# Roots of the down stage's first half taken ahead of its stores and of the next loads on GpSimd's queue

## The chip, the cores and the metric

The kernel runs on one core of one Trainium2 chip. The metric is the time of one execution on the device in microseconds (us), from the first instruction to the last; runs are compared by their median. The profile shows one further execution, taken instruction by instruction.

A core has five engines, each of which works through its own list of instructions in order: PE (TensorE, matrix products into the PSUM banks), DVE (VectorE), ACT (ScalarE), POOL (GpSimd) and SP (SyncE, which here only issues transfers). They wait for one another through semaphores. A DMA that an engine issues is carried out by the 16 DMA engines. SP's transfers stand in the profile as queue q1, POOL's as queue q0.

## The reference

A block of a language model in float32: 1024 rows of width 1024, a mixer of two branches, a feed-forward part with a short convolution, and a last normalisation. What matters here is its end:

```python
def rms_norm(x, g):
    xf = x.astype(jnp.float32)
    y = xf * lax.rsqrt(jnp.mean(xf * xf, axis=-1, keepdims=True) + EPS)
    return (y * g.astype(jnp.float32)).astype(x.dtype)

def conv_ffn(h, w_up, conv_w, conv_b, w_down):
    u = causal_dwconv(h @ w_up, conv_w, conv_b)
    gate, up = jnp.split(u, [D_FF], axis=-1)
    return (jax.nn.silu(gate) * up) @ w_down
...
    h = h + conv_ffn(rms_norm(h, norm_ffn[l]), ffn_w_up[l], ...)
    h = rms_norm(h, norm_final)
    return h[:, N_META:, :]
```

The last three lines are what the stage in question computes: the product with `w_down`, the sum with `h`, and the normalisation of each row.

## The kernel before

The kernel goes through its stages once: normalisation and projections, the heads of the two branches, their merge and the output product, the up product, and the down product with the final normalisation. Only the last one, the down stage, is touched.

**The down stage.** It multiplies the activations (1024 x 2816) by `w_down` (2816 x 1024) in a two-by-two block scheme with seven block products in place of eight. The rows of the output are made in two halves, r = 0 and r = 1. Each half has two phases, and each phase runs over 11 steps m; so there are 44 steps in the list `seq`, numbered 0 to 43. Step 22 is the first of the second half. In the first phase a step is 24 products of 128x128 by 128x512, eight groups of three, into the banks V, X, Y and Z for the row blocks j = 0 and j = 1. Steps 22 and 23 and steps 31 and 32 are run in pairs: j = 0 of both, and then j = 1 of both.

**Operands.** Each step has three operands: raw weights (`rd`), made weights (`tdn`) and activations (`adr`), in the first phase 512 KB each. `fill` (line 1732) fetches them with SP and splits each for the matrix unit into a rounded part (ACT, line 1752, `ACTIVATE`) and a rest (DVE, line 1753, `TENSOR_TENSOR`). The tile of a step is named by its home in memory, `db`, `do` or `dw`, and by the step's number: step 27 is `dw`, step 28 `db`, steps 29, 30 and 31 `do` with `dy` for the activations, step 32 `db` again. Eight homes are used in turn, so operands are fetched some steps ahead; a fetch waits until PE is through with the step whose home it takes.

**Rows.** The output rows of a half stand in four tiles `accs` of 128x1024. They come in from `hsc` (the values h), take up the banks' sums, and are normalised: `finish` (line 1849) adds the sums, squares (ACT, line 1858), makes the mean (DVE, `fv`, lines 1862 and 1864), the root (POOL, `fr`, line 1866, a power of -0.5), multiplies by the weights `gfin` (DVE, line 1871), scales by the root (ACT, line 1872) and stores the row block to `out` (line 1874). In the first half, roots, scaling and stores are put off: `later` keeps them until step 24, two steps into the second half, and the stores go out on POOL. The four loads of the next rows (`load_acc`, line 1838, POOL too) take the same four tiles, so each must wait until the store from its tile has landed.

**What sets the order.** The order on every engine is fixed when the program is built: instructions are taken by priority (`hp(n)` raises it) as their inputs are expected to be ready, so what is written in one loop is interleaved with the splitting of operands on ACT and DVE. `tc.issue_after(ins)` keeps what is issued inside it on `ins`'s engine behind `ins`.

Of the kernel before, what the change touches and what calls it, by code (L numbers as in the profile page):

```python
# [9 lines left out]
F32 = mybir.dt.float32  # L10
# [3 lines left out]
OP = mybir.AluOpType  # L14
# [3 lines left out]
P = 128  # L18
# [27 lines left out]
def hybrid_kernel(ctx, tc, x, meta, norm_mix, w_in, b_in, gla_w_gate, gla_b_gate, gla_norm,  # L46
                  ml_conv_w, ml_conv_b, ml_norm, w_branch_gla, w_branch_ml, w_out, norm_ffn,
                  ffn_w_up, ffn_conv_w, ffn_conv_b, ffn_w_down, norm_final, out):
    nc = tc.nc
    x, out = x[0], out[0]  # L50
# [8 lines left out]
    def hp(n):  # L59

        return tc.high_priority(offset=max(1, min(n, tc.cur_priority - floor[0])))

    const = ctx.enter_context(tc.tile_pool(name="const", bufs=1))
# [18 lines left out]
    mhalf = const.tile([P, 1], F32, name="mhalf")  # L82
# [5 lines left out]
    rooted, flipped = [], {}  # L88
# [79 lines left out]
    class Units:  # L168
# [3 lines left out]
        def add(self, *spec):  # L172
            self.specs.append(spec)
            return len(self.specs) - 1
# [166 lines left out]
    def norm_x(i):  # L341
        n = NM if i == 0 else P
        c0 = 0 if i == 0 else NM + P * (i - 1)
        xt = xts[i]
        ss = hd.tile([P, 1], F32, name=f"xss{i}", tag="ss1", bufs=3)
        junk = hd.tile([P, T], F32, name=f"xj{i}", tag="of", bufs=2)
        nc.scalar.activation(junk[:n, :D], xt[:n, :D], AF.Square, accum_out=ss[:n])
        with hp(40):
            v = hd.tile([P, 1], F32, name=f"xv{i}", tag="xv", bufs=3)
            nc.vector.tensor_scalar(v[:n], ss[:n], 1.0 / D, EPS, OP.mult, OP.add)  # L350
            rs = hd.tile([P, 1], F32, name=f"xr{i}", tag="xr", bufs=3)
            last = nc.gpsimd.tensor_tensor(rs[:n], v[:n], mhalf[:n], OP.pow)
        nc.vector.scalar_tensor_tensor(xt[:n, :D], xt[:n, :D], rs[:n], gmix[:n], OP.mult, OP.mult)
        for g in range(2):
            tp = ps.tile([P, 4, P], F32, name=f"xtp{i}_{g}", tag="pj" if i == 1 else "s", bufs=3)
            for j in range(4):
                k = 4 * g + j
                nc.tensor.transpose(tp[:, j, :n], xt[:n, k * P:(k + 1) * P], ident[:n, :n])
            with hp(40):
                h4 = xH[:, 4 * g:4 * g + 4, c0:c0 + n]  # L360
                rounded = nc.scalar.activation(h4, tp[:, :, :n], AF.Copy)
                l4 = xL[:, 4 * g:4 * g + 4, c0:c0 + n]
                nc.vector.tensor_tensor(l4, tp[:, :, :n], h4.bitcast(F32), OP.subtract)
        return last, rounded
# [38 lines left out]
    for i in range(5, NC + 1):  # L403
        last, _ = norm_x(i)
# [890 lines left out]
    def load_o(g, pool, tags, queue):  # L1295

        t = {}
        for p in "HL":
            for i in range(2):
                tag, shape = f"{tags}{p}{i}", [P, 4, NP]  # L1300
                t[p, i] = pool.tile(shape, F32R, name=f"o{g}{p}{i}", tag=tag)
        for k in range(NK):
            h, l = (t[p, k // 4][:, k % 4, :NP] for p in "HL")
            last = queue.dma_start(l.bitcast(F32), otd[g][k])
            split = nc.scalar.activation(h, l.bitcast(F32), AF.Copy)
            nc.vector.tensor_tensor(l, l.bitcast(F32), h.bitcast(F32), OP.subtract)
        return tuple([t[p, k // 4][:, k % 4, :] for k in range(NK)] for p in "HL"), last, split
# [43 lines left out]
    for j in range(NK):  # L1351
# [7 lines left out]
        if j == 1:  # L1359
            with tc.issue_after(opened.ins), tc.issue_after(loaded.ins):  # L1360
                om_, loaded, _ = load_o("m", r1b, "R", nc.gpsimd)
# [61 lines left out]
    for p in "HL":  # L1423
        t = rb.tile([P, 28, W0], F32R, name=f"B{p}0", tag=f"B{p}0")
# [403 lines left out]
    t = r2.tile([P, 4, D], F32, name="accs", tag="OL1")  # L1828
# [4 lines left out]
    def acc_of(r, j):  # L1833
        return accs[j], accs[2 + j]

    def load_acc(r, load, n):
        j, i = divmod(n, 2)
        return lambda: load(acc_of(r, j)[i], hsc[4 * i + 2 * r + j])
# [4 lines left out]
    def middle(r, j):  # L1843

        a, b = acc_of(r, j)
        with hp(400 if j == 0 else 200):
            for acc, h, x in ((a, lo, "X"), (b, hi, "Y"), (b, hi, "Z"), (a, lo, "V")):
                add(acc, h, banks[r, j, x])

    def finish(r, j):  # L1850
        acc = acc_of(r, j)
        end = (r, j) == (1, 1)
        if end:
            f0 = rb.tile([P, T], F32, name="f0", tag="T12")[:, :D]
        ss = [const.tile([P, 3], F32, name=f"fss{r}{j}{i}", tag=f"fs{i}", bufs=2) for i in range(2)]

        def square(i, n):
            return nc.scalar.activation(junk, acc[i][:, (lo, hi)[n]], AF.Square, accum_out=ss[i][:, n:n + 1])

        def root(i, cols=None):  # L1860
            v = const.tile([P, 1], F32, name=f"fv{r}{j}{i}", tag="hv", bufs=2)
            nc.vector.tensor_scalar(v, ss[i][:, i:i + 1], 1.0 / D, EPS, OP.mult, OP.add)
            for c in cols or [1 - i]:
                mean = nc.vector.scalar_tensor_tensor(v, ss[i][:, c:c + 1], 1.0 / D, v, OP.mult, OP.add)
            rs = const.tile([P, 1], F32, name=f"fr{r}{j}{i}", tag="hr", bufs=2)
            nc.gpsimd.tensor_tensor(rs, v, mhalf, OP.pow)
            return rs, mean

        def scaled(i):
            rs, _ = root(i)  # L1870
            nc.vector.tensor_tensor(acc[i], acc[i], gfin, OP.mult)
            nc.scalar.activation(acc[i], acc[i], AF.Copy, scale=rs)
            t = 4 * i + 2 * r + j
            (nc.sync if r else nc.gpsimd).dma_start(out[P * t:P * (t + 1), :], acc[i])

        with hp(400 if j == 0 else 200):
            for i, h in ((1, hi), (0, hi), (1, lo)):
                add(acc[i], h, banks[r, j, "X"])
            square(1, 1)
            square(0, 0)  # L1880
            if end:
                nc.vector.tensor_tensor(fo[:, hi], acc[1][:, hi], gfin[:, hi], OP.mult)
                nc.vector.tensor_tensor(f0[:, lo], acc[0][:, lo], gfin[:, lo], OP.mult)
            add(acc[0], hi, banks[r, j, "Y"])
            square(0, 1)
            if end:
                rs0, _ = root(0)
                nc.vector.tensor_tensor(f0[:, hi], acc[0][:, hi], gfin[:, hi], OP.mult)
            elif r:
                scaled(0)  # L1890
            if end:
                for c, q in zip((0, 2), QUARTERS):
                    nc.vector.tensor_tensor(acc[1][:, q], banks[r, j, "Z"][:, q], acc[1][:, q], OP.add)
                    squared = nc.scalar.activation(junk[:, q], acc[1][:, q], AF.Square, accum_out=ss[1][:, c:c + 1])
            else:
                add(acc[1], lo, banks[r, j, "Z"])
                square(1, 0)
                if r:
                    scaled(1)
                else:  # L1900
                    later.append(scaled)
                return
        with tc.issue_after(squared.ins):
            nc.scalar.activation(f0, f0, AF.Copy, scale=rs0)
        t = 2 * r + j
        nc.sync.dma_start(out[P * t:P * (t + 1), :], f0)
        rs, mean = root(1, (0, 2))
        with tc.issue_after(mean.ins):
            nc.vector.tensor_tensor(fo[:, lo], acc[1][:, lo], gfin[:, lo], OP.mult)
        t = NC - 1  # L1910
        nc.scalar.activation(fo[:, lo], fo[:, lo], AF.Copy, scale=rs)
        nc.scalar.dma_start(out[P * t:P * (t + 1), lo], fo[:, lo])
        nc.vector.tensor_scalar(fo[:, hi], fo[:, hi], rs, None, OP.mult)
        nc.sync.dma_start(out[P * t:P * (t + 1), hi], fo[:, hi])

    AHEAD, PRI_F, ACC_AT = 4, 100, 7
# [26 lines left out]
    back, later = [], []  # L1943
    i = FIRST
    while i < len(seq):
        r, ph, m = seq[i]
        k = i % NP2
        if k == 0 and ph == 0:
            open_round(r)

        n = 4 if (r, ph, k) == (1, 1, NP2 - 4) else 2 if k in (0, NP2 - 2) else 1
        ahead(i + n - 1)
        if later and k == 2:
            for whole in later:
                for x in range(2):
                    whole(x)
            later.clear()
        if (r, ph, k) == (1, 0, 5):
            with hp(PRI_F):
                for n4 in range(4):  # L1960
                    load_acc(r, nc.gpsimd.dma_start, n4)()
        end = i + n == len(seq)
        for j in range(2):
            if end and j:
                for b, c in (("X", lo), ("Y", lo), ("Z", QUARTERS[0]), ("Z", QUARTERS[1])):
                    for x in range(n):
                        down(i + x, j, b, c)
            else:
                for x in range(n):
                    down(i + x, j)  # L1970
            if k + n == NP2:
                (finish if ph else middle)(r, j)
        i += n
# [29 lines left out]
```

## Time and profile before

| | us |
|---|---|
| three runs | 1873.92, 1877.96, 1879.45 |
| median | 1877.96 |
| the profiled execution | 1881.06 |
| its span, first to last instruction | 1879.3 |
| PE busy in the span | 1848.5 (98%) |
| DVE busy | 1222.6 (65%) |
| ACT busy | 869.6 (46%) |
| POOL busy | 424.4 (23%) |

All times inside the profile count from the start of the span. The down stage's second half begins near 1755. A row of a timeline gives start, duration, engine, line, operation, result and sources, and in brackets the idle time of the engine just before and what ended it. A row of the windows gives the busy time of the engines in a stretch, then the clock granted to PE, the share of the DMA engines and their rate. A queue's row gives packets, MB, and the share of 16 engines that the packets took.

### The profile page before, as it was taken

The numbers are of one execution on the slowest core, as the hardware profiler recorded it, in microseconds if no ns is written. First come the engines' busy times: TensorE is split into PE (matmuls) and PEld (weight loads), VectorE is DVE, ScalarE is ACT, GpSimd is POOL, SyncE is SP. The second block draws the span as 40 slices with busy tenths as digits, with TensorE's granted clock in tenths as the row PEclk, the third lists the DMA queues.
The fourth block names the chain that finished last, engine by engine and source line by source line (L and its number), as shares of the span: only waits on it lengthen the run. The fifth ranks groups of instructions, "written<-read, shape, count | busy, mean of one in ns | idle before, by whom it ended". The sixth has DMA issues, their size and how long they took to land.

```text
span 1879.3 us, 32613 instructions
## 1 busy us (share of the span) xinstructions
PE 1848.5 (98%) x13284; PEld 1769.7 (94%) x13284; DVE 1222.6 (65%) x1813; ACT 869.6 (46%) x1395; POOL 424.4 (23%) x476
## 2 busy tenths in 40 slices
PE   8999999999999999999999999999999999999988
PEld 7899999999999999999999999999999999977866
DVE  7766756655552566655533547788878888787776
ACT  6565555645544434332512335444434434365664
POOL 5201101205441001142381600023222222100100
PEclk8999999999999999999999999999999999999999
DMA  5111022144223655665963733333333343298884
GB/s 176 52 37 60 24 60 60 46 104 138 86 88 108 191 146 145 176 173 165 350 217 118 233 131 113 113 118 118 103 112 109 107 129 118 79 373 296 285 325 165
DMA packets 221600, 270.08 MB, mean 144 GB/s; under 512 B 13870, under 2 KB 176737, under 8 KB 221451
## 3 DMA queue, kind: packets, MB, share of 16 engines
q1 hardware_dynamic: 200603, 196.76, 33.8%
q0 software_dynamic: 18336, 62.56, 10.0%
q10 hardware_dynamic: 2512, 8.68, 1.2%
q8 instruction: 104, 1.70, 0.4%
q14 instruction: 45, 0.37, 0.1%
HBM read 198.36 MB, written 69.60 MB: 143 GB/s over the span
## 4 chain that ended last, share of the span: by engine, by line
PE 83%; DVE 7%; DMA 4%; ACT 2%; issue 2%; POOL 1%; SPq 1%; POOLq 0%; ACTq 0%; DVEq 0%
PE pj L195 10%; PE pv L238 8%; PE Yu L1083 6%; PE Xu L1083 6%; PE Zu L1083 6%; PE bg L1322 5%; PE bm L1322 5%; PE Zg L1083 4%; PE Yg L1083 4%; PE Xg L1083 4%; PE po L1616 4%; PE Vu L1083 3%; PE pdX L1773 2%; PE pdZ L1773 2%; PE Vg L1083 2%; PE pdY L1773 2%
## 5 line engine op out<-in xcount | busy, mean ns | idle before, releaser
L546 POOL TENSOR_TENSOR ts<-ts 128x256 f32<-128x256 f32 x88 | 78.5, 897 | 46.1 <-DMA ts<-in_ffn_w_down_dram 43.9
L1529 POOL TENSOR_TENSOR SB<-SA,rg 128x512 f32<-128x512 f32 x20 | 34.4, 1720 | 238.6 <-issue 101.5
L238 PE MATMUL pv<-wH_mv,xH 128*128 128x256 f32 x256 | 74.8, 292 | 0.1
L238 PE MATMUL pv<-wH_gv,xH 128*128 128x256 f32 x256 | 74.4, 291 | 0.0
L788 POOL TENSOR_TENSOR pk<-pk,kT 128x256 f32<-128x256 f32 (+1 forms) x24 | 31.0, 1292 | 188.7 <-ACT pk L786 136.1
L1616 PE MATMUL po<-wH_wo,yH 128*128 128x256 f32 x256 | 72.6, 284 | 0.1
L1616 PE MATMUL po<-wL_wo,yH 128*128 128x256 f32 x256 | 71.9, 282 | 0.3 <-DVE wL_wo L112 0.3
L238 PE MATMUL pv<-wH_gv,xL 128*128 128x256 f32 x256 | 72.0, 281 | 0.0
L238 PE MATMUL pv<-wH_mv,xL 128*128 128x256 f32 x256 | 72.0, 281 | 0.0
L238 PE MATMUL pv<-wL_mv,xH 128*128 128x256 f32 x256 | 72.0, 281 | 0.0
L238 PE MATMUL pv<-wL_gv,xH 128*128 128x256 f32 x256 | 71.9, 281 | 0.0
L1616 PE MATMUL po<-wH_wo,yL 128*128 128x256 f32 x256 | 71.7, 281 | 0.0
L1564 DVE SCALAR_TENSOR_TENSOR cv<-u,fc,cv 128x1024 f32<-128x1024 f32 x44 | 65.2, 1484 | 0.4
L1511 POOL TENSOR_TENSOR A<-u2raw,A 128x512 fp32r<-128x512 f32 x20 | 43.0, 2150 | 85.2 <-ACT A L1510 85.2
L1322 PE MATMUL bg<-ogL,wH_bg 128*128 128x342 f32 x192 | 61.5, 320 | 0.0
L1322 PE MATMUL bm<-omH,wH_bm 128*128 128x342 f32 x192 | 61.4, 320 | 0.0
L1322 PE MATMUL bg<-ogH,wL_bg 128*128 128x342 f32 x192 | 61.4, 320 | 0.0
L1322 PE MATMUL bg<-ogH,wH_bg 128*128 128x342 f32 x192 | 61.4, 320 | 0.0
L1322 PE MATMUL bm<-omH,wL_bm 128*128 128x342 f32 x192 | 61.3, 319 | 0.0
L1322 PE MATMUL bm<-omL,wH_bm 128*128 128x342 f32 x192 | 61.2, 319 | 0.0
L242 DVE TENSOR_TENSOR v<-pv,bB 128x256 f32<-128x256 f32 x64 | 26.5, 418 | 39.3 <-PE pv L238 39.1
L1510 ACT ACTIVATE HA<-rg 128x1024 fp32r<-128x1024 f32 x16 | 17.0, 1061 | 72.8 <-PE Yu L1083 72.4
(787 smaller groups left out, 7515.6 us busy)
## 6 DMA issues: line engine op xcount, KB each, us to landing
gw<-in_w_in_dram SPq DMA_DIRECT2D x26, 512.0 KB
ts<-in_ffn_w_down_dram POOLq DMA_DIRECT2D x44, 256.0 KB, 3.8
tdn<-ts POOLq DMA_DIRECT2D x44, 256.0 KB, 3.0
rg<-in_ffn_w_up_dram SPq DMA_DIRECT2D x22, 512.0 KB
ru<-in_ffn_w_up_dram SPq DMA_DIRECT2D x22, 512.0 KB
adr<-s SPq DMA_DIRECT2D x40, 256.0 KB
rd<-in_ffn_w_down_dram SPq DMA_DIRECT2D x20, 512.0 KB
do<-tdn SPq DMA_DIRECT2D x18, 512.0 KB
```

What stands on the lines that cost most here:

```text
L195: nc.tensor.matmul(pt[:, :n], a[:, k, :], b[:, k, base + t0:base + t0 + n], start=(i == 0), stop=(i == 3 * NK - 1))
L238: nc.tensor.matmul(pt[:, :DV], a[:, k, t0:t0 + P], b[:, k % 4, :], start=(i == 0), stop=(i == 3 * NK - 1))
L242: nc.vector.tensor_tensor(vt[:n, c, :DV], pt[:n, :DV], bB[:n, :], OP.add)
L546: nc.gpsimd.tensor_tensor(t[:, o], t[:, a], t[:, b], OP.subtract)
L788: eng.tensor_tensor(e, e, k, OP.mult)
L1083: nc.tensor.matmul(out[:, :n], x[:, k, :], y[:, k, :], start=start and k == 0 and j == 0, stop=stop and k == 3 and j == 2, skip_group_chec ...
L1322: nc.tensor.matmul(pt[:, i, :n], a[:, k, :], b[k][:, base + t0:base + t0 + n], start=(k == 0 and j == 0), stop=(k == NK - 1 and j == 2))
L1511: eng.tensor_tensor(l, src, h.bitcast(F32), OP.subtract)
L1529: late.tensor_tensor(sb[:, 0:4], sa[:, 0:4], rg[:, 0:4], OP.subtract)
L1564: nc.vector.scalar_tensor_tensor(y, u[:, j:SEQ + j], fc[:, j, jj:jj + 1], y, OP.mult, OP.add)
L1616: nc.tensor.matmul(pt[:, :DV], a, b[:, k % 4, :], start=(k == 0 and i == 0), stop=(k == NK - 1 and i == len(terms) - 1))
L1773: nc.tensor.matmul(banks[r, j, b][:, c], p, q[:, c], start=first and k == 0, stop=last and k == 2, skip_group_check=True)
```

## The change

The roots of the four row blocks of the first half are written ahead of everything else: `later` holds `root` and `scaled` apart, all four roots are issued first, each into its own column of a new tile `first_roots`, and then the four row blocks are multiplied, scaled and stored, POOL's part (the stores) behind the last root. The four loads of the next rows are put behind the last store.

```diff
+    first_roots = const.tile([P, 4], F32, name="fr4")
...
-            rs = const.tile([P, 1], F32, name=f"fr{r}{j}{i}", tag="hr", bufs=2)
-            nc.gpsimd.tensor_tensor(rs, v, mhalf, OP.pow)
+            if r:
+                rs = const.tile([P, 1], F32, name=f"fr{r}{j}{i}", tag="hr", bufs=2)
+            else:
+                rs = first_roots[:, 2 * j + i:2 * j + i + 1]
+            rooted[:] = [nc.gpsimd.tensor_tensor(rs, v, mhalf, OP.pow)]
             return rs, mean
 
-        def scaled(i):
-            rs, _ = root(i)
+        def scaled(i, rs=None):
+            if rs is None:
+                rs, _ = root(i)
             nc.vector.tensor_tensor(acc[i], acc[i], gfin, OP.mult)
             nc.scalar.activation(acc[i], acc[i], AF.Copy, scale=rs)
             t = 4 * i + 2 * r + j
-            (nc.sync if r else nc.gpsimd).dma_start(out[P * t:P * (t + 1), :], acc[i])
+            return (nc.sync if r else nc.gpsimd).dma_start(out[P * t:P * (t + 1), :], acc[i])
...
-                    later.append(scaled)
+                    later.append((root, scaled))
...
         if later and k == 2:
-            for whole in later:
-                for x in range(2):
-                    whole(x)
+            ready = [(scaled, x, root(x)[0]) for root, scaled in later for x in range(2)]
+            with tc.issue_after(rooted[0].ins):
+                for scaled, x, rs in ready:
+                    stored = scaled(x, rs)
             later.clear()
         if (r, ph, k) == (1, 0, 5):
-            with hp(PRI_F):
+            with hp(PRI_F), tc.issue_after(stored.ins):
                 for n4 in range(4):
                     load_acc(r, nc.gpsimd.dma_start, n4)()
```

What this moves on the engines is not to be seen in the diff. On POOL, from the first root of the first half to the first root of the second (`fr000` to `fr011` are the four roots, `out_0_dram` the stores, `hsc` the loads), the order before is

```order
L1866 TENSOR_TENSOR fr000_18604<-fv000_18601,mhalf_81 128x1
L1874 DMA out_0_dram<-accs_17796 128x1024
L1866 TENSOR_TENSOR fr001_18612<-fv001_18609,mhalf_81 128x1
L1838 DMA accs_17796<-hsc_11183 128x1024
L1874 DMA out_0_dram<-accs_17796 128x1024
L1866 TENSOR_TENSOR fr010_18620<-fv010_18617,mhalf_81 128x1
L1838 DMA accs_17796<-hsc_11183 128x1024
L1874 DMA out_0_dram<-accs_17796 128x1024
L1866 TENSOR_TENSOR fr011_18628<-fv011_18625,mhalf_81 128x1
L1874 DMA out_0_dram<-accs_17796 128x1024
L1838 DMA accs_17796<-hsc_11183 128x1024 x2
```

and now

```order
L1871 TENSOR_TENSOR fr4_17800<-fv000_18602,mhalf_81 128x1
L1871 TENSOR_TENSOR fr4_17800<-fv001_18606,mhalf_81 128x1
L1871 TENSOR_TENSOR fr4_17800<-fv010_18610,mhalf_81 128x1
L1871 TENSOR_TENSOR fr4_17800<-fv011_18614,mhalf_81 128x1
L1880 DMA out_0_dram<-accs_17796 128x1024 x4
L1838 DMA accs_17796<-hsc_11183 128x1024 x4
```

Two of the four loads stood ahead of a root, and three of the four stores; now none does.

On ACT, around the same place (the scalings of `accs` between the roundings of steps 26, 27 and 28; `fr000` to `fr011` again), before:

```order
L1872 ACTIVATE accs_17796<-accs_17796,fr001_18612 128x1024
L1752 ACTIVATE dw270_18526<-rd27_18532 128x1024
L1752 ACTIVATE dw271_18527<-dw273_18529 128x1024
L1872 ACTIVATE accs_17796<-accs_17796,fr010_18620 128x1024
L1752 ACTIVATE dw274_18530<-dw275_18531 128x1024
L1752 ACTIVATE db28_18590<-rd28_18591 128x1024
L1752 ACTIVATE db28_18590<-db28_18590 128x1024
L1872 ACTIVATE accs_17796<-accs_17796,fr011_18628 128x1024
L1752 ACTIVATE db28_18590<-db28_18590 128x1024
```

and now

```order
L1878 ACTIVATE accs_17796<-accs_17796,fr4_17800 128x1024
L1752 ACTIVATE dw270_18527<-rd27_18533 128x1024
L1752 ACTIVATE dw271_18528<-dw273_18530 128x1024
L1878 ACTIVATE accs_17796<-accs_17796,fr4_17800 128x1024
L1752 ACTIVATE dw274_18531<-dw275_18532 128x1024
L1878 ACTIVATE accs_17796<-accs_17796,fr4_17800 128x1024
L1752 ACTIVATE db28_18591<-rd28_18592 128x1024
L1752 ACTIVATE db28_18591<-db28_18591 128x1024 x2
```

The last scaling has moved ahead of two more roundings of step 28; the other three stand where they stood.

On DVE the means (`fv`) of the same four row blocks stand between the multiplications by `gfin` and the splitting of steps 26 (`db26`) and 27 (`dw27`). From the second mean's end to the last one's, before:

```order
L1864 SCALAR_TENSOR_TENSOR fv001_18609<-fss001_18468,fv001_18609 128x1
L1753 TENSOR_TENSOR db26_18515<-db26_18515 128x1024
L1862 TENSOR_SCALAR fv010_18617<-fss010_18496 128x1
L1871 TENSOR_TENSOR accs_17796<-accs_17796,gfin_17797 128x1024
L1753 TENSOR_TENSOR dw272_18528<-rd27_18532,dw270_18526 128x1024
L1753 TENSOR_TENSOR dw273_18529<-dw273_18529,dw271_18527 128x1024
L1864 SCALAR_TENSOR_TENSOR fv010_18617<-fss010_18496,fv010_18617 128x1
L1862 TENSOR_SCALAR fv011_18625<-fss011_18497 128x1
L1871 TENSOR_TENSOR accs_17796<-accs_17796,gfin_17797 128x1024
L1864 SCALAR_TENSOR_TENSOR fv011_18625<-fss011_18497,fv011_18625 128x1
```

and now

```order
L1866 SCALAR_TENSOR_TENSOR fv001_18606<-fss001_18469,fv001_18606 128x1
L1864 TENSOR_SCALAR fv010_18610<-fss010_18497 128x1
L1877 TENSOR_TENSOR accs_17796<-accs_17796,gfin_17797 128x1024
L1753 TENSOR_TENSOR db26_18516<-db26_18516 128x1024 x2
L1866 SCALAR_TENSOR_TENSOR fv010_18610<-fss010_18497,fv010_18610 128x1
L1864 TENSOR_SCALAR fv011_18614<-fss011_18498 128x1
L1877 TENSOR_TENSOR accs_17796<-accs_17796,gfin_17797 128x1024
L1753 TENSOR_TENSOR dw272_18529<-rd27_18533,dw270_18527 128x1024
L1753 TENSOR_TENSOR dw273_18530<-dw273_18530,dw271_18528 128x1024
L1866 SCALAR_TENSOR_TENSOR fv011_18614<-fss011_18498,fv011_18614 128x1
```

The second mean's end has moved ahead of one more split of `db26`, the third one's ahead of both splits of `dw27`, the last one's ahead of one multiplication; it still stands behind the two splits of step 27. On PE and SP no row has moved.

## The prediction

> **What bounds the kernel now.** I read the table of windows first. The matrix unit (PE) is busy in nearly every microsecond of the second half of the down stage; the exception is one slice, and that slice lies just behind the moved work.
>
> ```profile
> 1640.00:1660.00 20.00, 18.21 (x101) 15.27 (x101) 17.34 (x20) 14.34 (x15) 0.00 (x0) 1.00 0.95 341
> ...
> 1780.00:1800.00 20.00, 13.98 (x51) 10.51 (x50) 8.79 (x8) 10.77 (x12) 2.24 (x4) 0.85 1.01 377
> 1800.00:1820.00 20.00, 20.00 (x87) 16.31 (x86) 15.36 (x16) 15.44 (x19) 1.07 (x2) 0.98 0.89 343
> ```
>
> Columns: stretch, its length, busy time of PE, weight load, DVE, ACT, POOL, granted PE clock, DMA share, GB/s. PE stands for 6.0 us in 1780 to 1800 and the clock falls to 0.85. Next the timeline of PE in that stretch, and two narrower windows of PE alone:
>
> ```profile
> 1783.10 0.86 PE L1773 MATMUL pdV<-dw,dw 128*128 128x512 f32 x3
> ...
> 1786.54 0.84 PE L1773 MATMUL pdX<-dw,dw 128*128 128x512 f32 x3
> ...
> 1787.90 0.84 PE L1773 MATMUL pdZ<-dw,dw 128*128 128x512 f32 x3
> 1794.73 2.05 PE L1773 MATMUL pdV<-db 128*128 128x512 f32 x3 [5.98 <-ACT db L1752]
> ...
> 1801.23 0.84 PE L1773 MATMUL pdX<-db 128*128 128x512 f32 x3
> ...
> 1794.73:1801.23 6.50, 6.46 (x16) 0.54 1.03 417
> ```
>
> Step 27 (dw) ends its issue at 1788.58 (1787.90 and one spacing of 0.68). Step 28 (db) could start there and starts at 1794.73, because ACT's rounding of its last operand is late. Then the clock is granted at 0.54, so that five groups take 6.50 us. Why ACT is late stands in its timeline and in POOL's:
>
> ```profile
> 1772.52 1.15 ACT L1872 ACTIVATE accs<-accs,fr 128x1024 f32<-128x1024 f32 x1 [2.76 <-POOL fr L1866]
> 1773.58 1.04 ACT L1752 ACTIVATE dw<-rd 128x1024 fp32r<-128x1024 f32 x1
> ...
> 1779.36 1.15 ACT L1872 ACTIVATE accs<-accs,fr 128x1024 f32<-128x1024 f32 x1 [3.78 <-POOL fr L1866]
> ...
> 1781.36 1.04 ACT L1752 ACTIVATE db<-rd 128x1024 fp32r<-128x1024 f32 x1
> 1782.31 1.04 ACT L1752 ACTIVATE db<-db 128x1024 fp32r<-128x1024 f32 x1
> 1792.58 1.15 ACT L1872 ACTIVATE accs<-accs,fr 128x1024 f32<-128x1024 f32 x1 [9.23 <-POOL fr L1866]
> 1793.63 1.04 ACT L1752 ACTIVATE db<-db 128x1024 fp32r<-128x1024 f32 x1
> ```
>
> ```profile
> 1768.16 0.59 POOL L1874 DMA_DIRECT2D out_dram<-accs  x1 [1.48 <-ACT accs L1872]
> 1771.02 1.47 POOL L1866 TENSOR_TENSOR fr<-fv,mhalf 128x1 f32<-128x1 f32 x1 [2.27 <-DVE fv L1864]
> 1777.63 0.59 POOL L1838 DMA_DIRECT2D accs<-hsc  x1 [5.14 <-DMA out_dram<-accs]
> 1778.21 0.53 POOL L1874 DMA_DIRECT2D out_dram<-accs  x1
> 1778.76 0.57 POOL L1866 TENSOR_TENSOR fr<-fv,mhalf 128x1 f32<-128x1 f32 x1
> 1790.86 0.58 POOL L1838 DMA_DIRECT2D accs<-hsc  x1 [11.54 <-DMA out_dram<-accs]
> 1791.43 0.53 POOL L1874 DMA_DIRECT2D out_dram<-accs  x1
> 1791.98 0.57 POOL L1866 TENSOR_TENSOR fr<-fv,mhalf 128x1 f32<-128x1 f32 x1
> ```
>
> POOL works in order. The load at 1790.86 waits 11.54 us for the second store to land, because it overwrites the row being stored, and the fourth root is queued behind that load. ACT's last scaling waits for that root (9.23 us), step 28's last rounding for the scaling, PE for the rounding. So a 0.6 us root carries the latency of a store to the matrix unit.
>
> **The change part by part.** Removed: loads and stores between the roots. POOL's queue is now four roots, four stores, four loads. Nothing is added but a tile of four columns; no instruction of PE, DVE, ACT or SP goes or comes, so no busy time changes.
>
> *The roots.* The last root now waits for DVE's last mean alone. That one stands behind two subtractions of step 27, which need ACT:
>
> ```profile
> 1774.65 1.23 DVE L1753 TENSOR_TENSOR dw<-rd,dw 128x1024 fp32r<-128x1024 f32 x1 [1.39 <-ACT dw L1752]
> 1775.80 1.22 DVE L1753 TENSOR_TENSOR dw<-dw,dw 128x1024 fp32r<-128x1024 f32 x1
> 1776.93 0.15 DVE L1864 SCALAR_TENSOR_TENSOR fv<-fss,fv 128x1 f32<-128x1 f32 x1
> ```
>
> Suppose none of this runs earlier than before (the second scaling, 2.3 us sooner or so, may pull it forward). Then the last mean ends at 1777.1 and the root, at the dearer of its two prices (1.47), at 1778.6. ACT scales the fourth row there instead of at 1792.58: 1.15 us, and then three roundings of step 28, some 0.95 apart and 1.04 long, end at 1782.6. In the new order the fourth scaling stands ahead of all three, which costs them 1.05 us each; that is in the count. Step 28 is due at 1788.58: 6.0 us of margin, and DVE's 1.22 behind it still fits. Step 28's first two operands had landed by 1781.36 and 1782.31 (no wait in their rows). The last one's landing is hidden behind the scaling; I bound it by its issue and the worst latency of the POOL queue:
>
> ```profile
> 1772.61 0.51 SPq L1729 DMA_DIRECT2D db<-adr  x1
> ...
> DMA to landing us min/median/max: 6.6/8.6/12.1
> ```
>
> At the worst 1784.7, and rounded by 1785.8, still before 1788.58. **So the wait goes: 6.15 us** (1794.73 less 1788.58), **and the slow clock behind it: 3.06 us** (6.50 for five groups, against 3.44 from 1783.10 to 1786.54). Together 9.21 us.
>
> *The transfers.* Four stores of 512 KB are now issued within some 2 us near 1779, and the loads follow as the stores land: 4.19 MB in POOL's queue q0 at a stretch, beside SP's operands in q1. What is late next? Three steps of eight groups at 0.69 put the paired steps 31 and 32 at 1805.1, and step 32, behind the first half of 31, at 1807.9. Its last operand and the traffic until then:
>
> ```profile
> 1805.82 1.06 ACT L1752 ACTIVATE db<-db 128x1024 fp32r<-128x1024 f32 x1 [0.48 <-DMA db<-adr]
> ...
> DMA packets 3615, 10.81 MB, mean 386 GB/s; under 512 B 339, under 2 KB 339, under 8 KB 3612
> q1 hardware_dynamic: 2780, 7.71, 73.2%
> q0 software_dynamic: 832, 3.06, 28.3%
> ...
> DMA packets 1057, 3.31 MB, mean 413 GB/s; under 512 B 105, under 2 KB 105, under 8 KB 1056
> q1 hardware_dynamic: 624, 1.72, 54.3%
> q0 software_dynamic: 432, 1.57, 48.6%
> ```
>
> The first three traffic rows are 1778 to 1806, the other three 1794 to 1802. Step 32's last operand landed at 1805.8, with 3.06 of q0's MB through since 1778. If all 4.19 go ahead of it, 1.13 MB more at 413 GB/s make it 2.7 us later, 1808.5. Rounded (1.06) and subtracted (1.22), it would let PE through at 1810.8, 2.9 us late. If the operands keep their place, it is not late at all; a gain below nothing is excluded, as PE has no other wait here. From 0 to 2.9 I take 1.0, since q1 kept over half (1.72 of 3.31 MB) in the fuller stretch. A wait of that size costs no clock: 1640 to 1660 has 1.8 us of PE idle at 1.00. The Trainium skill, "DMA: Bandwidth & Descriptors", Queues, rings and completion order, has each DMA engine go round between the queues that have work, packet by packet; the 1.72 beside 1.57 MB agrees. By that rule q0 would be through before 1805.8, the term would be 2.9 and the time 1.9 us above my forecast.
>
> The loads must land before the first sums of the second half, when step 32's first half is through, at 1810.7. At 1.57 MB in 8 us, q0's 4.19 MB take 21 us from 1780, to 1801; up to 9 us more is hidden under PE.
>
> *The sum.* 9.21 less 1.0 is 8.2 us. The profiled run took 1881.06 us, 1.76 around its span of 1879.3: 1872.9 from its own time. It lies 3.1 above the median of the runs shown (1877.96). If these lie elsewhere, the median becomes 1869.8; if they were part of this very wait, which hangs on a store's latency, 1872.9. I forecast **1870.5**, nearer to the first, since no row ties the 3.1 us to it.
>
> **The rivals.** *Given back at step 32.* The operand comes 2.9 us late and the clock falls as well, which costs up to the 3.06 seen here: 6.0 of the 9.2, a gain of 3.2, and 1874.8. For it: DMA is full from 1780 on (share 1.01). Against: the 1.8 us of idle at full clock.
>
> *Slower: a jam in the queues.* One stretch, 1780 to 1786, with a store and a load in q0, moved far less:
>
> ```profile
> DMA packets 500, 1.78 MB, mean 297 GB/s; under 512 B 44, under 2 KB 44, under 8 KB 500
> ```
>
> Were that the rate of all the bunched traffic, the 11.9 MB (10.81 and 1.13) would need 40 us from 1778, to 1818.2; step 32, 2.28 of split behind it, would start at 1820.5, 12.6 late, and 3.06 of slow clock would follow. 15.7 less 9.2 is 6.5 slower: 1884.5. It decides from a wait of 6.15 us at step 32 on, which is the operand landing at 1811.8, a mean below 353 GB/s. Against it stands 413 with two stores queued.
>
> *The root is no sooner.* Its mean needs step 27's roundings; were their operands 13 us later, the root would be back at 1792 and the time at 1878. ACT's 1773.58 without a wait speaks against it.
>
> **How the numbers follow.** Forecast 0.70, given back 0.17, root no sooner 0.04, jam 0.09. A measurement tells 0.3%, 5.6 us, from no change. The forecast's own range, 1867 to 1872.3, lies below the line of 1872.3; the second and third rivals lie within it, and the jam is over it (above 1883.6) in most of its cases: faster 0.70, same 0.23, slower 0.07. The range of 1866 to 1878 takes in the whole wait with some of the runs' spread below, and the give-back and the unmoved root above.
>
> **What would show it.** Right: four roots on POOL without a DMA between, done by 1779; ACT's waits for fr (2.76, 3.78 and 9.23) under 4 us together; no wait of PE before step 28; the window 1780 to 1800 at 20.0 and clock 1.00. Wrong in size: a PE wait at step 31 or 32 released by a DMA or by ACT behind one. Wrong altogether: roots finished after 1786, or under 353 GB/s between 1778 and 1812.

## The result and the profile after

| | before | after |
|---|---|---|
| median of 14 runs each, us | 1876.81 | 1871.68 |
| lowest to highest | 1873.64 to 1879.45 | 1869.44 to 1873.42 |
| ratio of the times, 95% interval | | 0.9976 (0.9969 to 0.9984) |
| the profiled execution | 1881.06 | 1872.98 |
| its span | 1879.3 | 1871.3 |

The kernel is 5.1 us faster by the medians, 0.24% by the ratio, with an interval clear of no change. The prediction drew its line between "faster" and "same" at 0.3%; the result falls on the side of "same", to which it gave 0.23. The two profiled executions differ by 8.1 us. The difference between these two numbers, 5.1 and 8.1, is the main question of what follows.

The windows of the kernel after, the same three stretches that were shown of before:

```profile
1640.00:1660.00 20.00, 19.02 (x114) 16.33 (x113) 17.93 (x20) 13.74 (x14) 0.00 (x0) 1.00 0.88 318
...
1780.00:1800.00 20.00, 20.00 (x89) 16.44 (x88) 9.79 (x9) 8.33 (x9) 2.13 (x4) 1.00 1.02 396
1800.00:1820.00 20.00, 20.00 (x87) 16.19 (x87) 19.34 (x23) 16.31 (x20) 0.00 (x0) 1.00 1.03 396
```

PE went from 13.98 to 20.00 us busy in 1780 to 1800, and its clock from 0.85 to 1.00. The timeline of POOL after:

```profile
1765.11 1.53 POOL L1871 TENSOR_TENSOR fr<-fv,mhalf 128x1 f32<-128x1 f32 x1 [88.53 <-DVE fv L1864]
...
1772.26 1.52 POOL L1871 TENSOR_TENSOR fr<-fv,mhalf 128x1 f32<-128x1 f32 x1 [2.11 <-DVE fv L1864]
1776.09 1.46 POOL L1871 TENSOR_TENSOR fr<-fv,mhalf 128x1 f32<-128x1 f32 x1 [2.31 <-DVE fv L1866]
1777.51 2.17 POOL L1880 DMA_DIRECT2D out_dram<-accs  x4
1782.14 0.54 POOL L1838 DMA_DIRECT2D accs<-hsc  x1 [2.46 <-DMA out_dram<-accs]
...
1790.22 0.53 POOL L1838 DMA_DIRECT2D accs<-hsc  x1 [1.16 <-DMA out_dram<-accs]
```

The fourth root ends at 1777.55, where it ended at 1792.55 before, and only DVE's means release the roots now. The loads still wait for stores, but no root is queued behind them. ACT's timeline and PE's show what came of it:

```profile
1777.58 1.15 ACT L1878 ACTIVATE accs<-accs,fr 128x1024 f32<-128x1024 f32 x1 [0.90 <-POOL fr L1871]
1778.64 1.04 ACT L1752 ACTIVATE db<-rd 128x1024 fp32r<-128x1024 f32 x1
1779.59 1.99 ACT L1752 ACTIVATE db<-db 128x1024 fp32r<-128x1024 f32 x2
...
1805.97 1.06 ACT L1752 ACTIVATE db<-db 128x1024 fp32r<-128x1024 f32 x1 [0.20 <-DMA db<-adr]
```

```profile
1789.06 0.85 PE L1773 MATMUL pdZ<-dw,dw 128*128 128x512 f32 x3
1789.75 0.85 PE L1773 MATMUL pdV<-db 128*128 128x512 f32 x3
...
1795.19 0.86 PE L1773 MATMUL pdV<-do,dy 128*128 128x512 f32 x3
```

Step 28's three roundings end at 1781.6 and PE reaches it at 1789.75, with no gap behind step 27. From the last group of step 27 to the first of step 29 PE takes 6.13 us; that is the yardstick for the other runs below. Step 32's last operand is rounded from 1805.97 on, against 1805.82 before, and PE enters that step without a wait.

### The profile page after: what moved, and what is told of

It is laid out like the page before. It is cut to its first block, busy times and chain, and to the rows that moved or that the text cites. A ratio compares the mean times of both kernels' runs of the same rounds, so it can differ in the third digit from the quotient of the medians.

```text
span 1871.3 us, 32608 instructions
## 1 busy us (share of the span) xinstructions
PE 1848.7 (99%) x13284; PEld 1771.3 (95%) x13284; DVE 1226.0 (66%) x1813; ACT 869.8 (46%) x1395; POOL 420.0 (22%) x476
```

## Six profiles of the kernel before

The first question was whether the 5.98 us wait of the first profile is what an ordinary execution has. The kernel before, unchanged, was profiled five times more.

> The kernel before, unchanged, profiled once more. The change took 8.0 us off the profiled span but only 5.1 us off the median of 14 runs, and the profiled run of before lay 4.2 us above its median. Theory A (the wait at step 28 swings from run to run, since it hangs on the landing of a store): PE's wait before step 28 will differ clearly from the 5.98 us of the first profile, likely 1 to 5 us, and the span will follow it, near 1879.3 less the difference. Theory B (the wait is always about 6 us and the changed kernel gives 3 to 4 us back where the profile does not show it): again 5.5 to 6.5 us of wait and the granted clock near 0.54 behind it, span 1878 to 1880.

> The kernel before, unchanged, a third profile, for the spread. Theory A: a third value of the wait before step 28, and over the three profiles span less wait agrees better than span alone. Theory B: 5.5 to 6.5 us again.

> The kernel before, unchanged, profiled once more. Three profiles of it so far give an own time of 1881.06, 1879.09 and 1878.40; from the moment TensorE is due at step 28 to the end of the slow groups they lose 9.2, 7.0 and 6.9 us, which leaves 1871.9, 1872.1 and 1871.5. Theory A (the spread of the kernel before is this one loss, and so is all of the gain): own time less that loss is 1871 to 1873 here too, and an execution under 1875 has no wait of TensorE before step 28 or one under 1 us. Rival F (the wait is there in every execution with about the same size, 3 us and more, and other stages make the spread): an execution under 1875 still waits 3 us, and the remainder falls under 1870.

> The same as for the profile before it: theory A leaves 1871 to 1873 behind the loss at step 28, whatever the own time is; rival F lets the remainder move with the own time.

> The same again: theory A leaves 1871 to 1873 behind the loss at step 28, whatever the own time is; rival F lets the remainder move with the own time.

The table takes from PE's timeline the start of the last group of step 27 and of the first group of step 29; their distance less 6.13 is what is lost at step 28, wait and slow clock together. "Own time" is the time of the profiled execution itself, "POOL" how long the second load waited for its store, "PE waits" how long PE waited for ACT's rounding (in e2 and e10 another 0.53 us for DVE's part follows).

| run | own time | POOL | PE waits | step 27's last, step 29's first | lost | own less lost |
|---|---|---|---|---|---|---|
| first profile | 1881.06 | 11.54 | 5.98 | 1787.90, 1803.27 | 9.24 | 1871.8 |
| e1 | 1879.09 | 9.91 | 4.34 | 1788.03, 1801.35 | 7.19 | 1871.9 |
| e2 | 1878.40 | 9.13 | 3.14 | 1787.43, 1800.67 | 7.11 | 1871.3 |
| e9 | 1880.21 | 9.32 | 3.30 | 1789.80, 1802.44 | 6.51 | 1873.7 |
| e11 | 1876.05 | 8.73 | 2.76 | 1787.35, 1798.32 | 4.84 | 1871.2 |
| e10 | 1873.28 | 7.35 | 0.60 | 1787.71, 1795.54 | 1.70 | 1871.6 |

The cheapest of them, e10, in POOL's and PE's timelines:

```profile
1785.28 0.58 POOL L1838 DMA_DIRECT2D accs<-hsc  x1 [7.35 <-DMA out_dram<-accs]
1785.86 0.53 POOL L1874 DMA_DIRECT2D out_dram<-accs  x1
1786.40 0.57 POOL L1866 TENSOR_TENSOR fr<-fv,mhalf 128x1 f32<-128x1 f32 x1
```

```profile
1787.71 0.84 PE L1773 MATMUL pdZ<-dw,dw 128*128 128x512 f32 x3
1789.15 0.73 PE L1773 MATMUL pdV<-db 128*128 128x512 f32 x2 [0.60 <-ACT db L1752]
1790.41 0.50 PE L1773 MATMUL pdV<-db 128*128 128x512 f32 x1 [0.53 <-DVE db L1753]
1790.75 0.86 PE L1773 MATMUL pdX<-db 128*128 128x512 f32 x3
```

It is the same queue with the same load ahead of the same root; the store was issued 1.4 us sooner and took 4.2 us less to land, and PE lost 1.7 us in place of 9.2. Five of the six remainders lie between 1871.2 and 1871.9, around the 1871.68 of the kernel after. The sixth, e9, is 0.7 above the 1871 to 1873 expected. It is the only one of the six whose clock falls in an earlier step too, near 1648 (1.00 in the same window of the other five):

```profile
1640.00:1660.00 20.00, 18.16 (x98) 15.40 (x97) 17.43 (x20) 14.04 (x15) 0.00 (x0) 0.91 0.89 325
```

When PE resumes there, e9 is 0.54 us behind e10 (1647.63 against 1647.09); at step 27's last group it is 2.09 us behind, which accounts for the difference of their remainders. So the loss at step 28 is never the same, from 1.7 to 9.2 us here, and it makes most of the spread of the kernel before, though not all of it. Theory B and rival F, a wait of much the same size in every execution, fall with e10. The median run, 1876.81, lies 5.1 above the kernel after, and the remainders agree with that kernel: an ordinary execution loses about that. The first profile was the dearest of six.

## Either half of the change alone

> The changed kernel without its second part: the loads of the next rows are no longer held behind the last store (on POOL: four roots, three stores, three loads, a store, a load). My theory (only what stands ahead of a root counts): no wait of PE at step 28, the last root done by 1779, time like the changed kernel's, 1869 to 1874, ratio 0.996 to 0.999. Rival (the bunching of the loads behind the last store is half of the gain): a PE wait of 2 us or more in 1780 to 1810 and a time of 1874 to 1877.

Against the kernel after, the loads are no longer held:

```diff
-            with hp(PRI_F), tc.issue_after(stored.ins):
+            with hp(PRI_F):
```

> The kernel before with the second part alone: roots, scalings and stores in turn as before, the four loads behind the last store. My theory (what holds the roots is the landing of a store that a load waits for, not the issue of a store): each root waits at most for ACT's scaling of the row before it, the last root is done by 1780, no wait of PE at step 28, 1869 to 1874. Rival (the roots must come ahead of the stores too): the last root after 1784, a PE wait of 2 us or more, 1874 to 1877.

Against the kernel before, the loads are held and the roots stay where they were:

```diff
-            (nc.sync if r else nc.gpsimd).dma_start(out[P * t:P * (t + 1), :], acc[i])
+            return (nc.sync if r else nc.gpsimd).dma_start(out[P * t:P * (t + 1), :], acc[i])
...
-                    whole(x)
+                    stored = whole(x)
...
-            with hp(PRI_F):
+            with hp(PRI_F), tc.issue_after(stored.ins):
```

| | median of runs | ratio to before (1877.81 there) |
|---|---|---|
| roots first only (e3) | 1872.77 of 12 | 0.9977 (0.9968 to 0.9986) |
| loads last only (e4) | 1872.44 of 11 | 0.9976 (0.9964 to 0.9987) |

Within these intervals each half gives as much as the whole (0.9976, in a batch of its own). With the roots first only, the last root ended at 1780.17, 1.2 us behind the 1779 expected, in an execution in which PE was due at step 28 only at 1792.01; PE did not wait there. POOL's timeline with the loads last alone:

```profile
1776.83 1.46 POOL L1866 TENSOR_TENSOR fr<-fv,mhalf 128x1 f32<-128x1 f32 x1 [2.69 <-DVE fv L1862]
1779.78 0.57 POOL L1874 DMA_DIRECT2D out_dram<-accs  x1 [1.48 <-ACT accs L1872]
1780.37 0.57 POOL L1866 TENSOR_TENSOR fr<-fv,mhalf 128x1 f32<-128x1 f32 x1
1782.71 0.57 POOL L1874 DMA_DIRECT2D out_dram<-accs  x1 [1.78 <-ACT accs L1872]
1783.28 1.07 POOL L1838 DMA_DIRECT2D accs<-hsc  x2
```

Three stores still stand between the roots, and each waits 1.5 us for its scaling, but none waits for a landing; the last root ends at 1780.94, 0.9 behind the 1780 expected, and PE stands nowhere in 1780 to 1820. What cost time was a load that waits for a store's landing with a root queued behind it. Moving the roots over it or it behind the roots comes to the same.

## The root made late on purpose

If the chain is root, scaling, rounding, PE, then a root that comes late for another reason must bring the loss back, and only beyond the margin. In three kernels a memset and two, six or eight products of 128x512 were put on POOL between the third and the fourth root, on a tile that is overwritten later:

```diff
-            rooted[:] = [nc.gpsimd.tensor_tensor(rs, v, mhalf, OP.pow)]
+            if (r, j, i) == (0, 1, 1):
+                spin = fo[:, :512]
+                with tc.issue_after(rooted[0].ins):
+                    nc.gpsimd.memset(spin, 1.0)
+                    for _ in range(2):
+                        spun = nc.gpsimd.tensor_tensor(spin, spin, spin, OP.mult)
+                with tc.issue_after(spun.ins):
+                    rooted[:] = [nc.gpsimd.tensor_tensor(rs, v, mhalf, OP.pow)]
+            else:
+                rooted[:] = [nc.gpsimd.tensor_tensor(rs, v, mhalf, OP.pow)]
```

> The kernel after with one memset and two products of 128x512 put on POOL between the third and the fourth root (on a tile that is overwritten later, so the output stays the same); nothing else moves. From the rows of the kernel after: the third root ends at 1773.78, products of 128x512 on POOL took about 1.6 us, so the fourth root starts near 1778.0 and not at 1776.09, 1.9 us later; the roundings of step 28 then end near 1783.5, and TensorE is due there at 1789.75. Theory A (the chain is root, ScalarE's scaling, the roundings behind it, TensorE; only what goes beyond step 28's due time costs): no wait of TensorE in 1780 to 1800, time as after, 1871 to 1873. Rival B (the four roots' nearness to each other is what gains, each us of root is a us of the end): about 1873.6 or more.

> The same with six products: the fourth root starts near 1784.4, 8.3 us later than in the kernel after; the roundings end near 1789.9, just at TensorE's due time of 1789.75. Theory A: a wait of 0 to 1.5 us, and a time between 1871.5 and 1876, according to whether so short a wait brings the clock down too. Rival B: 1880. Rival C (what cost before was the traffic of loads and stores in 1780 to 1800, not the place of the root): no wait and 1872.

> The same with eight products: the fourth root starts near 1787.6, 11.5 us later; the roundings end near 1793.1, 3.3 us beyond the due time. Theory A: TensorE waits 2.5 to 4.5 us before step 28, the granted clock of 1780 to 1800 falls to about 0.83 as in the kernel before, the groups behind it lose 2.5 to 3.8 us more, and the time is 1877 to 1879.5, as of the kernel before, though no load or store stands ahead of a root. Rival C: no wait, 1872. Rival B: 1883.

| products | fourth root starts | PE due at step 28 | lost at step 28 | clock in 1780 to 1800 | median, ratio to before (1876.82 there) |
|---|---|---|---|---|---|
| none (after) | 1776.09 | 1789.75 | 0 | 1.00 | 1871.68, its own batch |
| two (e5) | 1778.65 | 1790.17 | 0.0 | 1.00 | 1873.31, 0.9980 (0.9969 to 0.9992) |
| six (e6) | 1781.57 | 1786.86 | 0.6 | 1.00 | 1872.81, 0.9977 (0.9965 to 0.9989) |
| eight (e7) | 1787.76 | 1790.09 | 5.2 | 0.91 | 1876.11, 1.0003 (0.9989 to 1.0017) |

The starts alone can't be compared, since the profiled execution of e6, its fastest, reached step 28 some 3 us sooner than the others. Counted back from PE's due time, the root came 2.1, 8.4 and 11.3 us later than in the kernel after, where 1.9, 8.3 and 11.5 were expected.

PE's timeline with eight products:

```profile
1789.40 0.84 PE L1773 MATMUL pdZ<-dw,dw 128*128 128x512 f32 x3
1792.38 0.73 PE L1773 MATMUL pdV<-db 128*128 128x512 f32 x2 [2.13 <-ACT db L1752]
1794.02 0.50 PE L1773 MATMUL pdV<-db 128*128 128x512 f32 x1 [0.91 <-DVE db L1753]
1794.36 1.00 PE L1773 MATMUL pdX<-db 128*128 128x512 f32 x3
1795.16 1.48 PE L1773 MATMUL pdY<-db 128*128 128x512 f32 x3
...
1800.76 0.86 PE L1773 MATMUL pdV<-do,dy 128*128 128x512 f32 x3
```

The kernel with eight products is as slow as the kernel before, though neither a load nor a store stands ahead of a root: the lateness of the root alone is enough, and rival C (no wait, 1872) falls. With six products the root ends at 1782.11, 4.7 us ahead of PE's due time, and PE stands 0.35 us, within the 0 to 1.5 expected. The time is far from rival B's 1880, so it isn't each microsecond of the root that counts but what goes beyond PE's due time. Two products taken alone don't tell the two apart: 1873.31 lies between A's 1871 to 1873 and B's 1873.6 or more. With eight, the profiled execution took 1878.56, inside the 1877 to 1879.5 expected, but the median lies 0.9 below; the clock fell to 0.91 and not to 0.83, and the groups behind the wait lost 2.2 us, where 2.5 to 3.8 were expected. The medians of two and six products lie 1.6 and 1.1 above the kernel after, which was timed in another batch; whether any of that is the root isn't shown.

## The stores doubled

> The kernel after with each of the four stores of the closing rows issued twice to the same place, so that the queue of POOL moves 6.3 MB and not 4.2 MB in 1778 to 1812; the output stays the same. It tests the margin of step 32 in transfers, the term that the prediction put at 0 to 2.9 us and took as 1.0. 2.1 MB at the 396 GB/s of this stretch take 5.3 us. Theory D (the transfers have little margin there: step 32's last operand lands at 1805.95, its rounding ends at 1807.03 and TensorE is due at 1809.15, 2.1 us later): half to all of the 5.3 us reaches that operand, TensorE waits 0.5 to 3.2 us before step 32, and the time rises by 1 to 6 us to 1873 to 1878. Theory E (the loads of weights run ahead and give way, or the second loads land early enough): no wait, 1871.5 to 1873.

```diff
+            if not r:
+                nc.gpsimd.dma_start(out[P * t:P * (t + 1), :], acc[i])
             return (nc.sync if r else nc.gpsimd).dma_start(out[P * t:P * (t + 1), :], acc[i])
```

The median is 1877.6 (ratio to before 0.9999, 0.9989 to 1.0010), so the whole gain is lost and the time is as the first theory expected, but not at its place. POOL's timeline, and the waits of PE from 1700 on:

```profile
1788.10 0.53 POOL L1882 DMA_DIRECT2D out_dram<-accs  x1 [6.49 <-DMA out_dram<-accs]
...
1802.64 0.53 POOL L1882 DMA_DIRECT2D out_dram<-accs  x1 [8.72 <-DMA out_dram<-accs]
1803.17 1.58 POOL L1838 DMA_DIRECT2D accs<-hsc  x3
1809.48 0.53 POOL L1838 DMA_DIRECT2D accs<-hsc  x1 [4.74 <-DMA out_dram<-accs]
```

```profile
PE pdX L1773 <- DVE accs L1841: 3.5, 2, 2.7
```

Step 32's last operand landed 2.4 us later than in the kernel after (its rounding starts at 1808.39) and PE entered that step without a wait that the profile lists (its first group took 1.12 us in place of 0.85). But a second store to a place waits for the first one to land, so that the loads were issued as late as 1809.48; the sums (line 1841) that need them freed PE's banks late, and PE stood 2.7 and 0.8 us before the two halves of step 33. So both theories missed: the margin of the loads, not that of step 32, ran out first. The experiment doubled a chain of waits along with the traffic, and doesn't tell what the traffic alone would cost.

## Why the prediction came out as it did

**The wait and its chain: right.** Four roots without a DMA between them, done at 1777.55 (1778.6 forecast); no wait of PE at step 28; the window at 20.0 and 1.00. ACT's waits for roots are 1.1 us in all, where under 4 was forecast. The halves show that the load ahead of the root was the cause, and the late roots that the root's time decides.

**The size of the wait: right for the profiled execution, too large for the median one.** 9.21 us was measured correctly in one execution, the dearest of six. The step that failed is the choice behind the sum: "If these lie elsewhere, the median becomes 1869.8; if they were part of this very wait, which hangs on a store's latency, 1872.9. I forecast 1870.5, nearer to the first, since no row ties the 3.1 us to it." The 3.1 us were part of this very wait: in five of the six profiles, what the execution takes beyond 1871 to 1873 it loses there, and in e9 all but 0.7. The argument was already on the page (a store's latency ends the wait, and the runs before ranged over 5.5 us); what was missing was to follow it. The other end of the choice, 1872.9, is 1.2 above the measured median, and the forecast 1.2 below it; 1871.68 lies within the forecast's own range of 1867 to 1872.3. The gain forecast was 7.5 us, the one measured 5.1, so the line of 0.3%, 5.6 us, with a chance of 0.70 beyond it, was set near the most that the median execution had to give. Some of the closeness is luck. The choice drew the forecast 2.4 us down, the transfers' 1.0 us, which nothing measured bears out, drew it up, and the two errors partly cancel. The same holds for the profile's own time, where 1872.9 was forecast and 1872.98 taken: the kernel after lost nothing at step 32, but its profiled execution came to step 27 already 1.16 us later than the first profile of before (1784.26 against 1783.10), and was 1.43 us later near 1648, well ahead of all that was moved.

**The transfers: 1.0 us taken, nothing measured.** The traffic of the kernel after, three rows for 1778 to 1806 and one for 1760 to 1778, and then that of the kernel before in 1760 to 1778:

```profile
DMA packets 3626, 11.20 MB, mean 400 GB/s; under 512 B 349, under 2 KB 349, under 8 KB 3623
...
q1 hardware_dynamic: 2471, 6.97, 62.7%
q0 software_dynamic: 1152, 4.19, 39.5%
...
q1 hardware_dynamic: 2097, 5.99, 89.2%
```

```profile
q1 hardware_dynamic: 1847, 5.29, 82.9%
q0 software_dynamic: 144, 0.52, 7.1%
```

All of q0's 4.19 MB did go through before 1806, 1.13 more than before, as the dearer case had it, and q1 moved 0.74 MB less in that stretch. But it had moved 0.70 MB more in the 18 us ahead of it, in which no store went out before 1777.5 (before, q0 moved 0.52 MB there). The prediction counted what the bunched stores add to the traffic behind them and not what they no longer take from the traffic ahead of them: 5.99 and 6.97 make 12.96 MB for q1 by 1806, against 5.29 and 7.71 or 13.00 before. The margin left can be small: with two products in front of the fourth root, where the stores start 2.6 us later, PE does wait in step 32:

```profile
1810.47 0.50 PE L1773 MATMUL pdV<-db 128*128 128x512 f32 x1 [0.27 <-DVE db L1753]
```

With six and with eight products the stores start later still and PE doesn't wait there, so it isn't shown that the start of the stores sets this.

**The rivals.** The root came sooner, so that rival fell. Nothing was given back at step 32. The jam needed a mean below 353 GB/s; 1780 to 1786, the stretch that moved 297 before, moved 353 after, and the whole of 1778 to 1806 moved 400.

## What to carry to other kernels

A load that had to wait for a store to land held up, here for 5 to 12 us, everything behind it in the list of the engine that issues it; on an engine that also computes, move it behind the computation that others wait for, or that computation ahead of it. When a wait ends with a transfer's landing, its size in one profile is one draw: take several profiles, and set the sum against the runs' median, reading the spread of the runs as the spread of that wait, if nothing else in the profile varies. And traffic that is moved later leaves room where it was; count both sides.

## What was unexpected in the hardware

The landing of one and the same 512 KB store, at the same place in the program, kept POOL waiting from 7.35 to 11.54 us in six executions. Together with when the store was issued, that moved the loss at step 28 from 1.70 to 9.24 us.

The clock of PE answers a wait by a step rather than in proportion. Standing 0.60 and then 0.53 us (e10) left it at 1.00; 2.76 us (e11), or 2.13 and 0.91 (eight products), brought it down. How long PE stands doesn't decide it alone, as an earlier step shows that all these kernels have alike. First the kernel with eight products, PE's timeline and then the window:

```profile
1649.00 0.50 PE L1773 MATMUL pdV<-dy,dw 128*128 128x512 f32 x1 [1.60 <-ACT dw L1752]
1650.26 0.50 PE L1773 MATMUL pdV<-dy,dy 128*128 128x512 f32 x1 [0.52 <-DVE dy L1753]
```

```profile
1640.00:1660.00 20.00, 17.87 (x106) 15.46 (x106) 16.94 (x20) 13.71 (x14) 0.00 (x0) 1.00 0.87 311
```

Now e9, whose window of 0.91 was shown above:

```profile
1647.63 0.50 PE L1773 MATMUL pdV<-dy,dw 128*128 128x512 f32 x1 [1.31 <-ACT dw L1752]
1648.89 0.50 PE L1773 MATMUL pdV<-dy,dy 128*128 128x512 f32 x1 [0.54 <-DVE dy L1753]
```

It stood 0.27 us less, and there the clock fell. It also fell with the roots first only, at 1.78 and 0.54 us. The prediction's sentence that a wait of 1.8 us costs no clock was thus too sure: it holds in before's profile and not in e9's.

In narrow windows of PE alone the clock is either whole or half, and between 200 us and PE's last product each stretch of half clock lasts 3.41 or 6.83 us. The first row is that of the first profile of before at step 28, the next two are e9's 3.41 us ahead of the fall and its stretch of half clock near 1650, and the last is the kernel with eight products, whose clock stayed whole there:

```profile
1793.82:1800.65 6.83, 5.88 (x13) 0.50 1.03 412
...
1646.09:1649.50 3.41, 1.57 (x7) 1.00 1.04 398
1649.51:1652.92 3.41, 3.41 (x10) 0.50 1.04 416
...
1648.14:1651.56 3.42, 2.04 (x8) 1.00 1.04 414
```

If the time is cut into stretches of 3.41 us at the points where the clock changes, e9 stood 1.84 us within one of them; the kernel with eight products stood 2.12 us, but 1.38 at most within one. Over all profiles, from 200 us on and with the clock whole, a fall came behind each such stretch with 1.78 us or more of standing and behind none with up to 1.50; at 1.67 (before, 1787.00 to 1790.41) none came, at 1.66 (roots first only, 1648.20 to 1651.61) one did. So it may be the place of a wait against these stretches that decides. No run tests it.

The time at half clock isn't in proportion to the wait: 6.83 us behind 3.30 (e9) as behind 5.98, and 3.41 behind the 2.76 of e11:

```profile
1790.95 2.06 PE L1773 MATMUL pdV<-db 128*128 128x512 f32 x3 [2.76 <-ACT db L1752]
1792.81 1.48 PE L1773 MATMUL pdX<-db 128*128 128x512 f32 x3
1794.09 0.96 PE L1773 MATMUL pdY<-db 128*128 128x512 f32 x3
```

A group of 0.85 takes 1.48 us while the clock is down. The Trainium skill, "TensorE: Matmul & The Clock Gate", HAM oscillation, warns of gaps over about 3.4 us; here 2.76 us were enough, and 1.78 and 0.54 us in short succession.
